# Two widths of matmul, and a planned order, changed in a two-layer mixer block on one core

## The chip, the core and the metric

The kernel runs on one core of one Trainium2 chip. A core has a matrix engine (PE, with its weight loads shown apart as PEld), a vector engine (DVE), a scalar engine (ACT), GpSimd (POOL) and a queue engine (SP) that issues the DMAs here. The metric is device time in microseconds, from the start to the end of one execution; lower is better.

## What is computed

Two layers of a mixer block on 512 latent tokens and 256 context tokens, 1024 wide. Each layer projects the modulated input into three branches (retention `r`, gated MLP `m`, differential attention `d`), gates each branch, projects each back to 1024 columns, merges them with sigmoid gates and applies an output projection:

```
h  = modulate(rms_norm(x), shift, scale)
z  = h @ w_in                       # keys, values, queries, gates, u, v, merge logits
o_ret  = from_heads(rms_norm(bidir_retention(rq, rk, rv)))  * silu(rg)
o_diff = from_heads(rms_norm(diff_attend(dq, dk, dv, lam))) * silu(dg)
o_mlp  = mu * spatial_mix(layer_norm(mv)) * silu(mg)
y   = sigmoid(l_r)*(o_ret @ w_bo[0]) + sigmoid(l_m)*(o_mlp @ w_bo[1]) + sigmoid(l_d)*(o_diff @ w_bo[2])
x   = x + gate * rms_norm(y @ w_out, g_post)
```

In layer 0 all 768 tokens go through everything. In layer 1 the context tokens only give keys and values, so most stages there have 512 tokens.

## The kernel before

Every projection is a product of two float32 numbers that are each kept as a high and a low part in a rounded 32-bit type (`HH` and `HL` for the input, a ring of two slots for weights). One product is therefore three matmuls per 128 rows of the contraction: high by high, high by low, low by high. All of them are recorded from line 314.

There are two kinds of projection. In `xs` tokens are the stationary side: one call makes 128 tokens by 256 output columns, with 24 matmuls of 256 columns. In `ws` weights are the stationary side: 128 output channels by a span of tokens. The gates (`dg`, `rg`), the merges (`dm`, `rm`, `mm`), and `mg` and `mu` of the gated MLP use `ws`. In layer 0 such a call is made for two spans, tokens 512 to 767 first (matmuls of 256 columns) and then tokens 0 to 511 (512 columns). A merge step has 36 matmuls for each span (24 for the logits, 12 for the branch), a gate step 24. `spans`, `cm_tiles`, `gate`, `merge` and `mlp` hold this.

The `v` projection of the gated MLP (`mv0`, `mv1`, columns 0 to 255 and 256 to 511) goes through `main_pairs`, first all token tiles with `mv0`, then all with `mv1`. The output projection (`out_phase`) takes four blocks of 256 columns, `wo0` to `wo3`, one after the other for each token tile.

Weights are loaded by `w_dma` into one of two raw buffers and divided by `w_split` into high and low part, in four pieces of 512 words: one ACT copy and one DVE subtraction each. `begin` splits a block and, ahead of time, the next one. Results lie in the eight PSUM banks of 512 words.

The attention and retention units (`d_unit`, tags `dat`; `r_state` and `r_attn`, tags `rst` and `rat`) are small matmuls with long chains on ACT and DVE between them. They are put in a list of side work and taken from it by `pop`, between the projections. One attention unit writes scores into the three banks `Sb`; DVE takes their maximum (`red`, line 370), ACT makes two exponentials from them, and only then may the next unit write its scores.

The order on each engine is not the order of the code. `Rec` records every operation with a cost; `schedule` plans time with these costs and with `LATENCY`, the time from an engine's end to another's start, and at each moment gives an engine the ready operation with the lowest place in the code (`prio`, which `bump` shifts). Engines then run strictly in that planned order.

Of the kernel before, what the change touches and what calls it, by code (L numbers as in the profile page):

```python
# [12 lines left out]
ALU = mybir.AluOpType  # L13
# [3 lines left out]
NT = NL + NCX  # L17
# [169 lines left out]
class Op:  # L187
# [4 lines left out]
LATENCY = {("PE", "ACT"): 200, ("PE", "DVE"): 200, ("PE", "SP"): 200, ("ACT", "PE"): 290, ("ACT", "DVE"): 100, ("ACT", "POOL"): 100,  # L192
           ("ACT", "SP"): 100, ("ACT", "ACT"): 100, ("DVE", "PE"): 290, ("DVE", "ACT"): 150, ("DVE", "POOL"): 170, ("DVE", "DVE"): 127,
           ("DVE", "SP"): 100, ("POOL", "PE"): 150, ("POOL", "ACT"): 65, ("POOL", "DVE"): 65, ("POOL", "POOL"): 102, ("POOL", "SP"): 100}
# [4 lines left out]
class Rec:  # L199
# [144 lines left out]
    def copy_v(self, out, in_):  # L344
        v = self.nc.vector
        c = self.n(in_) / (0.96 if self.ps(in_) or self.ps(out) else 1.92) + 160
        return self.add("DVE", lambda: v.tensor_copy(out, in_), [out], [in_], c)

    def tt(self, out, a, b, op):
        v = self.nc.vector  # L350
        return self.add("DVE", lambda: v.tensor_tensor(out, a, b, op=op), [out], [a, b], self.n(out) / 0.97 + 168)  # L351

    def ts(self, out, a, s1, s2=None, op0=ALU.mult, op1=None):
        v = self.nc.vector
        ins = [a] + [s for s in (s1, s2) if s is not None and not isinstance(s, float)]
        c = self.n(out) * (1.04 if self.ps(a) else 0.52) + 160 + 60 * (len(ins) - 1)
        if op1 is None:
            f = lambda: v.tensor_scalar(out, a, s1, None, op0=op0)  # L358
        else:
            f = lambda: v.tensor_scalar(out, a, s1, s2, op0=op0, op1=op1)  # L360
        return self.add("DVE", f, [out], ins, c)

    def stt(self, out, a, s, b, op0, op1):
        v = self.nc.vector
        ins = [a, b] + ([] if isinstance(s, float) else [s])
        return self.add("DVE", lambda: v.scalar_tensor_tensor(out, a, s, b, op0=op0, op1=op1), [out], ins, self.n(out) / 0.97 + 215)  # L366

# [12 lines left out]
    def bn_stats(self, out, in_):  # L380
        v = self.nc.vector
        return self.add("DVE", lambda: v.bn_stats(out, in_), [out], [in_], self.n(in_) / 0.96 + 155)

    def bn_aggr(self, out, in_):
        v = self.nc.vector
        return self.add("DVE", lambda: v.bn_aggr(out, in_), [out], [in_], 172)

    def ptt(self, out, a, b, op):
        g = self.nc.gpsimd
        n = self.n(out)  # L390
        c = 600 + 150 * n if op == ALU.pow else 2.4 * n + 250
        return self.add("POOL", lambda: g.tensor_tensor(out, a, b, op=op), [out], [a, b], c)  # L392
# [169 lines left out]
WBUMP = -20  # L562
H_LO = 6144
# [7 lines left out]
class Prog:  # L571
# [444 lines left out]
    def h_unit(self, k, ts_, v):  # L1016
# [408 lines left out]
    def cm_tiles(self, l, W, X, n0, ps):  # L1425

        if ps[1] is not None:
            self.ws(ps[1], X, slice(NL, NT), W, n0)
        self.ws(ps[0], X, slice(0, NL), W, n0)

    def spans(self, l):
        return ((0, 0, NL), (1, NL, NT)) if l == 0 else ((0, 0, NL),)
# [6 lines left out]
    def gate(self, l, c):  # L1439
# [5 lines left out]
        for i in range(2):  # L1445
            self.begin(l, f"{c}g{i}")
            W = self.W(l, f"{c}g{i}")
            for j in range(2):
                ch = 2 * i + j
                R.tag = f"L{l}.{c}g{ch}"  # L1450
                ps = [self.P(NL), self.P(NCX, align=256) if l == 0 else None]
                self.cm_tiles(l, W, (self.HH, self.HL), 128 * j, [p.ap if p else None for p in ps])
# [12 lines left out]
    def merge(self, l, c, extra=None):  # L1465
# [9 lines left out]
        for i in range(8):  # L1475
# [4 lines left out]
            ps = [self.P(NL), None, self.P(NL), None]  # L1480
            x = None
            if l == 0:
                x = self.P(2, NCX)
                ps[1], ps[3] = _View(x[:, 0]), _View(x[:, 1])
# [3 lines left out]
            for v, a, b in reversed(self.spans(l)):  # L1488
                R.tag = f"L{l}.{c}m{i}"
                self.ws(ps[v].ap, (self.HH, self.HL), slice(a, b), Wl, 0)  # L1490
                self.ws(ps[2 + v].ap, self.OT, slice(a, b), Wb, 0)
                R.tag += ".ev"
                R.act(sg[:, a:b], ps[v].ap, AF.Sigmoid)
                R.tt(dst[:, a:b], ps[2 + v].ap, sg[:, a:b], ALU.mult)
# [15 lines left out]
    def mlp(self, l):  # L1510
# [7 lines left out]
        vn = [F(512) for _ in range(nt)]  # L1518
        for i in range(2):
# [32 lines left out]
        for i in range(2):  # L1552
            self.begin(l, f"mu{i}")
            W = self.W(l, f"mu{i}")
            for j in range(2):
                g = 2 * i + j
                R.tag = f"L{l}.mu{g}"
                sp = [self.P(NL), self.P(NCX, align=256) if l == 0 else None]
                ps = [self.P(NL), self.P(NCX, align=256) if l == 0 else None]
                with R.pe():  # L1560
                    for t in range(nt):
                        o = sp[0][:, 128 * t:128 * t + 128] if t < 4 else sp[1][:, 128 * (t - 4):128 * (t - 4) + 128]
                        R.mm(o, vn[t][:, 128 * g:128 * g + 128], wst[:, g], True, True)
                self.cm_tiles(l, W, (self.HH, self.HL), 128 * j, [p.ap if p else None for p in ps])
# [58 lines left out]
    def out_phase(self, l):  # L1623
# [5 lines left out]
        for gi, g in enumerate(gs):  # L1629
# [7 lines left out]
            if gi == 0:  # L1637
                pss = [self.P(DM, hi=3072), self.P(DM, hi=3072)]
                for b in range(4):
# [17 lines left out]
            else:  # L1657
                for j, t in enumerate(g):
                    end = t == gs[-1][1]
                    if end and last:  # L1660

                        ps = self.P(3, 512)
                        pq = [ps[:, (0, 0, 1, 2)[b], 256 * (b == 1):256 * (b == 1) + 256] for b in range(4)]
                    else:
                        ps = self.P(DM, lo=1024 if end else 0, hi=3072)
                        pq = [ps[:, 256 * b:256 * b + 256] for b in range(4)]
                    for b in range(4):
                        R.tag = f"L{l}.out{t}"
                        self.xs(pq[b], (yh, yl), slice(128 * j, 128 * j + 128), wos[b])
# [4 lines left out]
                    if end and last:  # L1674
                        self.tile_last(l, t, ps, [(ps[:, 0], 0, 512), (pq[2], 512, 768), (pq[3], 768, 1024)])
# [189 lines left out]
```

## Time and profile before

| | us |
|---|---|
| median of 3 runs (1535.66 to 1537.17) | 1536.49 |
| the profiled execution, whole | 1536.63 |
| its span, first to last instruction | 1534.9 |
| PE busy | 1505.0 |
| DVE busy | 799.0 |
| ACT busy | 602.3 |

An engine's busy time is the union of its instructions' shown lengths. A matmul's shown length is longer than its share of the engine's time, since matmuls are pipelined: their starts lie closer together than their ends suggest. What a matmul costs is read from the distance of starts. The page's sections and the answers of the trace name groups by line, engine, operation and tile; `AR` holds high and low parts, `AF` plain float32, `PSM` the PSUM.

### The profile page before, as it was taken

What the parts mean: (1) busy time and instruction counts of PE and PEld (TensorE: products, weight loads), DVE (VectorE), ACT (ScalarE), POOL (GpSimd) and SP (SyncE); (2) the same over time, 40 slices, a digit from 0 to 9 for tenths busy, and PEclk for the clock granted to TensorE, in tenths of its full rate; (3) what the DMA queues carried; (4) which work ended last, traced back from release to release, by engine and by line L of the source; (5) the groups of instructions that cost most, each with busy time, mean ns of one, the idle gap of its engine ahead of it and who ended that gap; (6) DMA issues with size and microseconds to landing.
All of it is one profiled execution on the core that took longest, in us unless ns stands there. A gap on an engine that the chain in (4) does not pass through costs nothing.

```text
span 1534.9 us, 23633 instructions
## 1 busy us (share of the span) xinstructions
PE 1505.0 (98%) x9544; PEld 1350.8 (88%) x9544; DVE 799.0 (52%) x1551; ACT 602.3 (39%) x1298; POOL 168.9 (11%) x187
## 2 busy tenths in 40 slices
PE   7999999999999999999999999999999999999998
PEld 4799998989888888989889999989988888898888
DVE  4457635655333872235874654674656434344452
ACT  6735543573222222222223463464455333332341
POOL 1212201110000011001000131111110000201000
PEclk9999999999999999999999999999999999999999
DMA  9441312111231442122563223241211332321331
GB/s 364 144 138 56 86 40 76 50 52 63 75 116 54 165 138 83 56 74 88 187 201 124 97 101 121 86 117 49 83 42 56 103 117 83 118 98 65 119 124 69
DMA packets 37710, 156.32 MB, mean 102 GB/s; under 512 B 5345, under 2 KB 6497, under 8 KB 31201
## 3 DMA queue, kind: packets, MB, share of 16 engines
q1 hardware_dynamic: 37600, 154.81, 30.0%
q8 instruction: 75, 1.23, 0.3%
q14 instruction: 35, 0.28, 0.1%
HBM read 132.77 MB, written 4.19 MB: 89 GB/s over the span
## 4 chain that ended last, share of the span: by engine, by line
PE 94%; issue 1%; DVE 1%; ACT 1%; DMA 0%; POOL 0%; SPq 0%; DVEq 0%; POOLq 0%; ACTq 0%
PE PSM L314 91%; PE PSM L318 3%; ACT AF L339 1%; DMA AF<-AF 0%; POOL AF L392 0%; DVE AR L351 0%; SPq L401 0%; DVE AF L351 0%; DVE AF L366 0%; DVE AF L370 0%; ACT AR L339 0%; DVE AF L360 0%; DVE AF L378 0%; DVEq L1861 0%; POOLq L1861 0%
## 5 line engine op out<-in xcount | busy, mean ns | idle before, releaser
L314 PE MATMUL PSM<-AR 128*128 128x256 f32 (+1 forms) x8016 | 1361.8, 330 | 9.1 <-ACT AF L339 7.3
L314 PEld LDWEIGHTS PSM<-AR 128*128 128x128 f32 x8016 | 1186.5, 190 | 140.7 <-ACT AF L339 9.6
L339 ACT ACTIVATE AR<-AF 128x512 fp32r<-128x512 f32 (+4 forms) x489 | 285.2, 607 | 422.3 <-PE PSM L314 295.9
L351 DVE TENSOR_TENSOR AR<-AF,AR 128x512 fp32r<-128x512 f32 (+4 forms) x486 | 318.6, 673 | 252.6 <-ACT AR L339 205.2
L339 ACT ACTIVATE AF<-PSM 128x512 f32<-128x512 f32 (+4 forms) x385 | 170.5, 462 | 392.1 <-PE PSM L314 324.3
L392 POOL TENSOR_TENSOR AF<-AF 128x1 f32<-128x1 f32 (+5 forms) x180 | 168.2, 943 | 1360.9 <-DVE AF L360 588.5
L351 DVE TENSOR_TENSOR AF<-PSM,AF 128x512 f32<-128x512 f32 (+2 forms) x253 | 144.7, 581 | 236.6 <-PE PSM L314 111.8
L314 PE MATMUL PSM<-AF 128*128 128x128 f32 (+3 forms) x1104 | 143.9, 304 | 12.4 <-DMA AF<-wmodn 8.9
L314 PEld LDWEIGHTS PSM<-AF 128*128 128x128 f32 (+1 forms) x1104 | 127.2, 184 | 23.9 <-DVE AF L360 9.3
L339 ACT ACTIVATE AF<-PSM,AF 128x768 f32<-128x768 f32 (+2 forms) x144 | 91.9, 648 | 64.9 <-DVE AF L358 40.5
L374 DVE CUSTOM_DVE_ANT_0 AR<-AF 128x1024 fp32r<-128x1024 f32 x59 | 76.5, 1296 | 14.8 <-DMA AF<-wmod 8.8
L370 DVE TENSOR_REDUCE AF<-PSM 128x2 f32<-128x1536 f32 (+1 forms) x40 | 61.4, 1541 | 35.7 <-PE PSM L314 35.6
L360 DVE TENSOR_SCALAR AF<-AF 128x1 f32<-128x1 f32 (+3 forms) x188 | 42.5, 237 | 61.5 <-ACT AF L339 58.3
L318 PE MATMUL PSM<-AF 128*128 128x128 f32 x424 | 67.5, 277 | 2.1 <-DVE AF L366 1.2
L339 ACT ACTIVATE AF<-AF 128x256 f32<-128x256 f32 (+4 forms) x107 | 54.7, 558 | 20.4 <-POOL AF L392 10.3
L318 PEld LDWEIGHTS PSM<-AF 128*128 128x128 f32 x424 | 51.2, 142 | 13.1 <-ACT AF L339 3.2
L351 DVE TENSOR_TENSOR AF<-AF 128x512 f32<-128x512 f32 (+5 forms) x78 | 42.9, 555 | 13.2 <-PE PSM L318 5.0
L366 DVE SCALAR_TENSOR_TENSOR AF<-AF 128x768 f32<-128x768 f32 (+2 forms) x48 | 43.5, 913 | 3.6 <-POOL AF L392 2.7
L366 DVE SCALAR_TENSOR_TENSOR AF<-AF,PSM 128x128 f32<-128x128 f32 x64 | 19.8, 344 | 20.5 <-PE PSM L314 12.0
L358 DVE TENSOR_SCALAR AF<-AF 128x2 f32<-128x2 f32 (+4 forms) x98 | 20.4, 223 | 7.0 <-PE PSM L314 3.4
L360 DVE TENSOR_SCALAR AF<-PSM,AF 128x128 f32<-128x128 f32 x48 | 15.9, 404 | 12.0 <-PE PSM L318 11.9
L351 DVE TENSOR_TENSOR AR<-PSM,AR 64x256 fp32r<-64x256 f32 x24 | 10.1, 421 | 21.2 <-ACT AR L339 21.0
(20 smaller groups left out, 94.3 us busy)
## 6 DMA issues: line engine op xcount, KB each, us to landing
AF<-w SPq DMA_DIRECT2D x50, 1024.0 KB, 4.8
AF<-w SPq DMA_DIRECT2D x48, 768.0 KB, 4.2
AF<-wmod SPq DMA_DIRECT2D x32, 512.0 KB, 3.6
AF<-wmodn SPq DMA_DIRECT2D x16, 512.0 KB, 8.9
AF<-x SPq DMA_DIRECT2D x12, 512.0 KB, 4.2
AR<-AR SPq DMA_DIRECT2D x16, 384.0 KB, 4.6
AF<-AF SPq DMA_DIRECT2D x64, 64.0 KB, 2.3
AR<-AF SPq DMA_DIRECT2D x12, 256.0 KB, 2.3
```

Source lines behind the costliest of these rows:

```text
L314: self.add("PE", lambda: pe.matmul(out, lhsT, rhs, start=start, stop=stop), [out], [lhsT, rhs], c)
L318: self.add("PE", lambda: pe.transpose(out, in_, ident), [out], [in_, ident], 109.0)
L339: return self.add("ACT", lambda: e.activation(out, in_, func, **kw), outs, ins, c, tab)
L351: return self.add("DVE", lambda: v.tensor_tensor(out, a, b, op=op), [out], [a, b], self.n(out) / 0.97 + 168)
L358: f = lambda: v.tensor_scalar(out, a, s1, None, op0=op0)
L360: f = lambda: v.tensor_scalar(out, a, s1, s2, op0=op0, op1=op1)
L366: return self.add("DVE", lambda: v.scalar_tensor_tensor(out, a, s, b, op0=op0, op1=op1), [out], ins, self.n(out) / 0.97 + 215)
L370: return self.add("DVE", lambda: v.tensor_reduce(out, in_, axis=AX.X, op=op), [out], [in_], self.n(in_) / 0.96 + 155)
L374: return self.add("DVE", lambda: v.tensor_tensor_reduce(junk, a, b, 1.0, 0.0, ALU.mult, ALU.add, accum), [junk, accum], [a, b], self.n(a) ...
L392: return self.add("POOL", lambda: g.tensor_tensor(out, a, b, op=op), [out], [a, b], c)
```

## The change

Five things are changed.

1. In layer 0 the spans of `ws` are tokens 0 to 383 and 384 to 767, so that all its matmuls have 384 columns. Each span has a bank of its own (`banks`).
2. `v` projection: the first pair of token tiles is done as before, with `mv0` and then `mv1`; every further tile is done at once for both, with matmuls of 512 columns. Their moving side are two halves of 256 words from the two ring slots (`w_both`). `mv1` no longer splits the next block ahead, since that block's slot is still in use; the last tile is recorded in four groups of two rows of the contraction.
3. Output projection: blocks 0 and 1, and 2 and 3, are taken together in 512 columns in the same way, but for the first pair's blocks 0 and 1 and for the last tile's blocks 2 and 3.
4. The costs in `Rec` and the table `LATENCY` have new numbers: costs are smaller by 40 to 150 ns, the times from ACT or DVE to PE by 137 and 153 ns.
5. Side work is recorded with `ABUMP = -100`, which lets its operations go ahead of up to 100 others in the planner's choice.

```diff
-LATENCY = {("PE", "ACT"): 200, ("PE", "DVE"): 200, ("PE", "SP"): 200, ("ACT", "PE"): 290, ("ACT", "DVE"): 100, ("ACT", "POOL"): 100,
+LATENCY = {("PE", "ACT"): 200, ("PE", "DVE"): 200, ("PE", "SP"): 200, ("ACT", "PE"): 153, ("ACT", "DVE"): 133, ("ACT", "POOL"): 177,
...
-        c = self.n(in_) / 1.19 + (160 if self.ps(in_) else 195) + 198 * (accum is not None) + 60 * (len(ins) - 1)
+        c = self.n(in_) / 1.19 + (60 if self.ps(in_) else 95) + 150 * (accum is not None) + 88 * (len(ins) - 1)
...
+ABUMP = -100
...
-            self.w_split(i + 1)
+            if name != "mv1":
+                self.w_split(i + 1)
...
+        self.R.bump = ABUMP
         f()
+        self.R.bump = 0
...
+    def w_both(self, off, step):
+        a = self.AR[:, off:off + 2 * step].rearrange("p (a b) -> p a b", a=2)[:, :, 0:2048]
+        return a.rearrange("p a (k n) -> p k a n", k=KT)
...
+        for v, a, b in reversed(self.spans(l)):
+            self.ws(ps[v].ap, X, slice(a, b), W, n0)
+
+    def banks(self, l):
+        return [self.P(b - a, align=512) for v, a, b in self.spans(l)]
 
     def spans(self, l):
-        return ((0, 0, NL), (1, NL, NT)) if l == 0 else ((0, 0, NL),)
+        return ((0, 0, NT // 2), (1, NT // 2, NT)) if l == 0 else ((0, 0, NL),)
...
-            self.main_pairs(l, f"mv{i}", PAIRS if l == 0 else LATP, post)
+            self.main_pairs(l, f"mv{i}", prs[:1], post)
+        W = [self.w_both(RING[0] + 2048 * i, RING[1] - RING[0]) for i in range(2)]
+        for t in [t for pr in prs[1:] for t in pr]:
+            R.tag = f"L{l}.mv.{t}"
+            ps = self.P(2, 256)
+            for k in (0, 2, 4, 6) if t == prs[-1][1] else (None,):
+                self.xs(ps.ap, (self.HH, self.HL), slice(128 * t, 128 * t + 128), W, k if k is None else (k, k + 2))
+            R.copy_a(vn[t].ap, ps.ap.rearrange("p a b -> p (a b)"))
...
+                half = [[self.w_both(RING[0] + 2048 * x, RING[1] - RING[0]) for x in range(2)],
+                        [self.w_both(Z + 6144 * x, 2048) for x in range(2)]]
...
+                    if b == 2:
+                        continue
...
-                            self.xs(pss[j][:, 256 * b:256 * b + 256], (yh, yl), slice(128 * j, 128 * j + 128), wos[b], ks)
+                            o = pss[j][:, 512:1024].rearrange("p (a b) -> p a b", a=2) if b == 3 else pss[j][:, 256 * b:256 * b + 256]
+                            self.xs(o, (yh, yl), slice(128 * j, 128 * j + 128), half[1] if b == 3 else wos[b], ks)
```

What stands on PE at two places follows. In these rows `AR` matmuls belong to projections, or to the scores of an attention unit where they come as 2, 4 and 2; L318 are transposes, and `AF` matmuls of L314 products of the attention units or of retention.

PE in layer 0, late in the attention of head 3, before: the scores of one unit (the rows 512, 256, 256, 512), and from the eighth row on the scores of the next.

```order
L314 MATMUL PSM<-AR 128x512 x2
L314 MATMUL PSM<-AR 128x256 x2
L318 MATMUL PSM<-AF 128x128
L314 MATMUL PSM<-AF 128x128 x2
L314 MATMUL PSM<-AR 128x256 x2
L314 MATMUL PSM<-AR 128x512 x2
L318 MATMUL PSM<-AF 128x128 x8
L314 MATMUL PSM<-AR 128x512 x2
L314 MATMUL PSM<-AR 128x256 x2
```

The same two units of the same head on PE in the changed kernel:

```order
L314 MATMUL PSM<-AR 128x512 x2
L314 MATMUL PSM<-AR 128x256 x4
L314 MATMUL PSM<-AR 128x512 x2
L314 MATMUL PSM<-AR 128x256 x24
L318 MATMUL PSM<-AF 128x128
L314 MATMUL PSM<-AF 128x128 x6
L314 MATMUL PSM<-AR 128x256 x24
L318 MATMUL PSM<-AF 128x128 x7
L314 MATMUL PSM<-AR 128x512 x2
L314 MATMUL PSM<-AR 128x256 x4
L314 MATMUL PSM<-AR 128x512 x2
```

Between the two units' scores stood eight transposes; now there stand two projections of 24 matmuls, eight transposes and six products.

PE at the end of layer 0 before: the last merge step (36 and 36), the output projection, and in between the transposes (eight for a token tile) that bring a finished tile into the next layer.

```order
L314 MATMUL PSM<-AR 128x256 x36
L314 MATMUL PSM<-AR 128x512 x36
L314 MATMUL PSM<-AR 128x256 x264
L318 MATMUL PSM<-AF 128x128 x8
L314 MATMUL PSM<-AR 128x256 x24
L318 MATMUL PSM<-AF 128x128 x4
L314 MATMUL PSM<-AR 128x256 x24
L318 MATMUL PSM<-AF 128x128 x4
L314 MATMUL PSM<-AR 128x256 x72
L318 MATMUL PSM<-AF 128x128 x8
```

The same place in the changed kernel:

```order
L314 MATMUL PSM<-AR 128x384 x132
L314 MATMUL PSM<-AR 128x256 x96
L314 MATMUL PSM<-AR 128x512 x72
L318 MATMUL PSM<-AF 128x128 x8
L314 MATMUL PSM<-AR 128x512 x24
L318 MATMUL PSM<-AF 128x128 x8
L314 MATMUL PSM<-AR 128x512 x48
L318 MATMUL PSM<-AF 128x128 x8
```

The merge runs in one width, and the output projection in 512 columns after its first 96 matmuls.

## Rows read from the trace of the kernel before

**Rows 1.** The page: busy time and share by engine; granted clock, 40 slices.

```profile
PE 1505.0 (98%) x9544; PEld 1350.8 (88%) x9544; DVE 799.0 (52%) x1551; ACT 602.3 (39%) x1298; POOL 168.9 (11%) x187
...
PEclk9999999999999999999999999999999999999999
```

**Rows 2.** Groups by form on PE, whole span: busy us, mean ns; idle.

```profile
L314 PE MATMUL PSM<-AR 128*128 128x512 f32 x3344 | 799.3, 393 | 3.6 <-ACT AF L339 3.6
L314 PE MATMUL PSM<-AR 128*128 128x256 f32 x4672 | 590.3, 284 | 5.5 <-ACT AF L339 3.7 <-DVE AF L351 1.6
```

**Rows 3.** The same view of 618 to 646 us, and of 1205 to 1250.

```profile
L314 PE MATMUL PSM<-AR 128*128 128x256 f32 x236 | 28.5, 283 | 0.0
...
L314 PE MATMUL PSM<-AR 128*128 128x512 f32 x200 | 45.5, 389 | 0.0
```

**Rows 4.** The same view, at 522.59 (256 after 512) and 526.90 (512 after 256).

```profile
L314 PE MATMUL PSM<-AR 128*128 128x256 f32 x1 | 0.3, 278 | 0.0
...
L314 PE MATMUL PSM<-AR 128*128 128x512 f32 x1 | 0.4, 396 | 0.0
```

**Rows 5.** Timeline of PE, first stage (two halves of 256): start us, us.

```profile
42.65 1.64 PE L314 MATMUL PSM<-AR 128*128 128x512 f32 x6
...
44.48 2.32 PE L314 MATMUL PSM<-AR 128*128 128x512 f32 x9
```

**Rows 6.** Waits of PE, 60 to 1200 us: us in total, times, longest.

```profile
PE PSM L314 <- ACT AF L339: 9.1, 8, 2.5
PE PSM L314 <- DVE AF L351: 1.6, 1, 1.6
PE PSM L318 <- DVE AF L366: 1.2, 3, 0.5
PE PSM L318 <- ACT AF L339: 0.5, 1, 0.5
```

**Rows 7.** Timeline at 308 us, attention of layer 0, head 3; idle in brackets.

```profile
308.30 1.04 PE L318 MATMUL PSM<-AF 128*128 128x128 f32 x8
308.50 1.76 DVE L370 TENSOR_REDUCE AF<-PSM 128x2 f32<-128x1536 f32 x1 [1.52 <-PE PSM L314]
...
310.79 0.91 ACT L339 ACTIVATE AF<-PSM,AF 128x768 f32<-128x768 f32 x1
...
311.85 0.97 PE L314 MATMUL PSM<-AR 128*128 128x512 f32 x4 [2.51 <-ACT AF L339]
```

**Rows 8.** Timeline of PE, attention of layer 1, head 3.

```profile
1139.48 1.39 PE L314 MATMUL PSM<-AR 128*128 128x512 f32 x4 [1.12 <-ACT AF L339]
...
1143.77 1.60 PE L314 MATMUL PSM<-AF 128*128 128x128 f32 x12 [0.90 <-ACT AF L339]
...
1147.34 1.13 PE L318 MATMUL PSM<-AF 128*128 128x128 f32 x7 [0.37 <-DVE AF L366]
```

**Rows 9.** Timeline of PE, attention of layer 1, head 1.

```profile
1030.62 0.97 PE L314 MATMUL PSM<-AR 128*128 128x256 f32 x4 [1.08 <-ACT AF L339]
...
1033.95 1.60 PE L314 MATMUL PSM<-AF 128*128 128x128 f32 x12 [0.90 <-ACT AF L339]
```

**Rows 10.** Timeline of ACT, end of layer 0: finishing tile 4, and weight pieces.

```profile
844.91 1.02 ACT L339 ACTIVATE AF<-PSM 128x1024 f32<-128x1024 f32 x1 [11.61 <-PE PSM L314]
...
848.80 1.02 ACT L339 ACTIVATE AR<-AF 128x256 fp32r<-128x256 f32 x3
...
850.77 1.63 ACT L339 ACTIVATE AR<-AF 128x256 fp32r<-128x256 f32 x5
...
853.39 2.10 ACT L339 ACTIVATE AF<-AF 128x1024 f32<-128x1024 f32 x2 [0.99 <-POOL AF L392]
```

**Rows 11.** The page: two costliest groups of weight splitting; DMA of weight blocks.

```profile
L339 ACT ACTIVATE AR<-AF 128x512 fp32r<-128x512 f32 (+4 forms) x489 | 285.2, 607 | 422.3 <-PE PSM L314 295.9
L351 DVE TENSOR_TENSOR AR<-AF,AR 128x512 fp32r<-128x512 f32 (+4 forms) x486 | 318.6, 673 | 252.6 <-ACT AR L339 205.2
...
AF<-w SPq DMA_DIRECT2D x50, 1024.0 KB, 4.8
```

More of the change, by code (lines that the diff above doesn't have):

```diff
@@ L188 @@
     pass
-LATENCY = {("PE", "ACT"): 200, ("PE", "DVE"): 200, ("PE", "SP"): 200, ("ACT", "PE"): 290, ("ACT", "DVE"): 100, ("ACT", "POOL"): 100,
-           ("ACT", "SP"): 100, ("ACT", "ACT"): 100, ("DVE", "PE"): 290, ("DVE", "ACT"): 150, ("DVE", "POOL"): 170, ("DVE", "DVE"): 127,
-           ("DVE", "SP"): 100, ("POOL", "PE"): 150, ("POOL", "ACT"): 65, ("POOL", "DVE"): 65, ("POOL", "POOL"): 102, ("POOL", "SP"): 100}
+LATENCY = {("PE", "ACT"): 200, ("PE", "DVE"): 200, ("PE", "SP"): 200, ("ACT", "PE"): 153, ("ACT", "DVE"): 133, ("ACT", "POOL"): 177,
+           ("ACT", "SP"): 135, ("ACT", "ACT"): 135, ("DVE", "PE"): 137, ("DVE", "ACT"): 119, ("DVE", "POOL"): 163, ("DVE", "DVE"): 117,
+           ("DVE", "SP"): 117, ("POOL", "PE"): 93, ("POOL", "ACT"): 73, ("POOL", "DVE"): 73, ("POOL", "POOL"): 102, ("POOL", "SP"): 100}
 WINDOW = 3413.3
@@ L345, in copy_v @@
         v = self.nc.vector
-        c = self.n(in_) / (0.96 if self.ps(in_) or self.ps(out) else 1.92) + 160
+        c = self.n(in_) / (0.96 if self.ps(in_) or self.ps(out) else 1.92) + 76
         return self.add("DVE", lambda: v.tensor_copy(out, in_), [out], [in_], c)
@@ L350, in tt @@
         v = self.nc.vector
-        return self.add("DVE", lambda: v.tensor_tensor(out, a, b, op=op), [out], [a, b], self.n(out) / 0.97 + 168)
+        return self.add("DVE", lambda: v.tensor_tensor(out, a, b, op=op), [out], [a, b], self.n(out) / 0.97 + 84)
     def ts(self, out, a, s1, s2=None, op0=ALU.mult, op1=None):
@@ L355, in ts @@
         ins = [a] + [s for s in (s1, s2) if s is not None and not isinstance(s, float)]
-        c = self.n(out) * (1.04 if self.ps(a) else 0.52) + 160 + 60 * (len(ins) - 1)
+        c = self.n(out) * (1.04 if self.ps(a) else 0.52) + 76 + 60 * (len(ins) - 1)
         if op1 is None:
@@ L390, in ptt @@
         n = self.n(out)
-        c = 600 + 150 * n if op == ALU.pow else 2.4 * n + 250
+        c = 560 + 150 * n if op == ALU.pow else 2.4 * n + 210
         return self.add("POOL", lambda: g.tensor_tensor(out, a, b, op=op), [out], [a, b], c)
@@ L1450, in gate @@
                 R.tag = f"L{l}.{c}g{ch}"
-                ps = [self.P(NL), self.P(NCX, align=256) if l == 0 else None]
-                self.cm_tiles(l, W, (self.HH, self.HL), 128 * j, [p.ap if p else None for p in ps])
+                ps = self.banks(l)
+                self.cm_tiles(l, W, (self.HH, self.HL), 128 * j, ps)
                 sg = F(n)
@@ L1479, in merge @@
             Wb = self.W(l, f"{c}m{i}", 128, 1024, 4)
[L1480 to L1484, printed above, removed]
+            ps, pb = self.banks(l), self.banks(l)
             sg = F(n)
@@ L1490, in merge @@
                 self.ws(ps[v].ap, (self.HH, self.HL), slice(a, b), Wl, 0)
-                self.ws(ps[2 + v].ap, self.OT, slice(a, b), Wb, 0)
+                self.ws(pb[v].ap, self.OT, slice(a, b), Wb, 0)
                 R.tag += ".ev"
                 R.act(sg[:, a:b], ps[v].ap, AF.Sigmoid)
-                R.tt(dst[:, a:b], ps[2 + v].ap, sg[:, a:b], ALU.mult)
+                R.tt(dst[:, a:b], pb[v].ap, sg[:, a:b], ALU.mult)
                 if last:
@@ L1501, in merge @@
             sg.free()
-            for p in (ps[0], ps[2], x):
-                if p is not None:
-                    p.free()
+            for p in (*ps, *pb):
+                p.free()
             if extra:
@@ L1518, in mlp @@
         vn = [F(512) for _ in range(nt)]
+        prs = PAIRS if l == 0 else LATP
         for i in range(2):
@@ L1522, in post @@
                     R.copy_a(vn[t][:, 256 * i:256 * i + 256], ps[:, j])
-            self.main_pairs(l, f"mv{i}", PAIRS if l == 0 else LATP, post)
+            self.main_pairs(l, f"mv{i}", prs[:1], post)
[6 more added lines that the diff above has]
+            R.copy_a(vn[t].ap, ps.ap.rearrange("p a b -> p (a b)"))
+            ps.free()
+            self.step()
         R.tag = f"L{l}.ln"
@@ L1540, in mlp @@
                 R.tag = f"L{l}.mg{2 * i + j}"
-                ps = [self.P(NL), self.P(NCX, align=256) if l == 0 else None]
-                self.cm_tiles(l, W, (self.HH, self.HL), 128 * j, [p.ap if p else None for p in ps])
+                ps = self.banks(l)
+                self.cm_tiles(l, W, (self.HH, self.HL), 128 * j, ps)
                 s = F(n)
@@ L1557, in mlp @@
                 R.tag = f"L{l}.mu{g}"
-                sp = [self.P(NL), self.P(NCX, align=256) if l == 0 else None]
-                ps = [self.P(NL), self.P(NCX, align=256) if l == 0 else None]
+                sp, ps = self.banks(l), self.banks(l)
                 with R.pe():
                     for t in range(nt):
-                        o = sp[0][:, 128 * t:128 * t + 128] if t < 4 else sp[1][:, 128 * (t - 4):128 * (t - 4) + 128]
+                        v, a, b = self.spans(l)[t // 3 if l == 0 else 0]
+                        o = sp[v][:, 128 * t - a:128 * t - a + 128]
                         R.mm(o, vn[t][:, 128 * g:128 * g + 128], wst[:, g], True, True)
-                self.cm_tiles(l, W, (self.HH, self.HL), 128 * j, [p.ap if p else None for p in ps])
+                self.cm_tiles(l, W, (self.HH, self.HL), 128 * j, ps)
                 f = F(n)
@@ L1662, in out_phase @@
                         ps = self.P(3, 512)
-                        pq = [ps[:, (0, 0, 1, 2)[b], 256 * (b == 1):256 * (b == 1) + 256] for b in range(4)]
+                        po = [(ps[:, 0].rearrange("p (a b) -> p a b", a=2), half[0]), (ps[:, 1, 0:256], wos[2]), (ps[:, 2, 0:256], wos[3])]
                     else:
                         ps = self.P(DM, lo=1024 if end else 0, hi=3072)
-                        pq = [ps[:, 256 * b:256 * b + 256] for b in range(4)]
-                    for b in range(4):
+                        po = [(ps[:, 512 * b:512 * b + 512].rearrange("p (a b) -> p a b", a=2), half[b]) for b in range(2)]
+                    for b, (o, w) in enumerate(po):
                         R.tag = f"L{l}.out{t}"
-                        self.xs(pq[b], (yh, yl), slice(128 * j, 128 * j + 128), wos[b])
+                        self.xs(o, (yh, yl), slice(128 * j, 128 * j + 128), w)
                         if end and not last and b == 0:
```

17 lines of the change are left out of this document (7 added, 10 removed).

## The prediction

> **What bounds the kernel now.** I read the page first. PE is busy for 1505.0 of 1534.9 us, no other engine for more than about half, and the granted clock is full in all 40 slices, that is 2.4 GHz [rows 1]. So time can only go where PE spends it: in the number and width of its matmuls, or in the gaps between them. Two forms make up nearly all of it, 4672 matmuls of 256 columns and 3344 of 512 [rows 2]. Their lengths overlap, so the cost is the distance of starts: in a stretch of one form, busy time less one length, over the count less one. That is (28.5 - 0.283)/235 = 120.0 ns for 256 columns and (45.5 - 0.389)/199 = 226.7 ns for 512 [rows 3]. The two forms come to 560.6 + 758.1 = 1319 us. One column costs less in a wide matmul: 0.443 ns against 0.469.
>
> The gaps are few. Between 60 and 1200 us PE is seen waiting 13 times, 12.4 us in all [rows 6]. A gap only shows once it outlasts the overlap of two bars, 283 - 120 = 163 ns, so 13 x 0.163 = 2.1 us are hidden and the waits are worth about 14.5 us. All of the large ones lie in the two attention stretches. Outside them nothing waits, so other engines' work in merges and gates is hidden.
>
> **The change part by part.** The sum is made against the profiled execution, 1536.6 us, which is 0.1 us from the median of the runs.
>
> *256 to 512 columns.* `v` projection: 96 matmuls fewer in layer 0 (four tiles), 48 in layer 1 (two tiles). Output projection: 48 + 192 in layer 0 (first pair, four tiles), 48 + 48 + 24 in layer 1 (first pair, a tile, half of the last). Together 504 fewer. Each replaces 2 x 120.0 by 226.7, if two halves of 256 words stream like one piece of 512. The first stage has such matmuls already: three more of them take 2.32 - 1.64 = 0.68 us, 227 ns each [rows 5]. The gain is 504 x 13.3 ns = **6.7 us**. The rows are rounded to 10 ns, 3 ns over three matmuls, which gives 5 to 8.4 us.
>
> *512 and 256 to 384 columns.* 24 merge steps of 36, eight gate steps of 24, eight steps each of 24 in `mg` and `mu` (four and four channels): 864 + 192 + 192 = 1248 pairs. A pair costs 226.7 + 120.0 = 346.7 ns now. No row has a matmul of 384, so its cost lies between the neighbours, 120.0 and 226.7, which would be a gain or a loss of up to 1248 x 106.7 = 133 us. The straight line between the two points gives 173.3 and no gain; 512's price per column gives 170.0 and a gain of 6.7 ns a pair. I take 170.0, for this reason. A matmul of 256 in a row of its like is shown with 283 ns, the first one behind a matmul of 512 with 278 [rows 3, 4]. The first 512 behind 256s is shown with 396, one in a row of 512s with 389. So something that a predecessor of 226.7 covers and one of 120.0 doesn't (the weight load, which goes beside it) adds 5 to 7 ns. Without it 256 columns would cost about 113, which is 512's price per column. A 384 has a predecessor of 170, well over 120, and should be free of it. Gain: 1248 x 6.7 ns = **8.3 us**, with 0 as the near bound.
>
> On the length of a bar the Trainium skill says (Perfetto Trace Analysis, the section on the Tensor Engine under "Per-instruction lifecycle") that a matmul's start is the start of its operand fetch and its end an estimate. By that the 5 to 7 ns are partly a model; no sum changes, but the straight line keeps a fair chance.
>
> *The waits.* The largest is of this kind: the next attention unit's scores need DVE's maximum (1.76 us) and ACT's exponential (0.91) of the last, 3.4 us from 308.5 to 311.85, while only eight transposes (1.04) stand between: 2.51 us idle [rows 7]. In the new order there stand 48 matmuls of 256 (5.8 us), eight transposes (0.9) and six products (1.3): 8.0 us for the same 3.4. The next place is head 3 of layer 1, 1.12 + 0.90 + 0.37 [rows 8]; the new order puts 48 matmuls of a projection between those scores. Head 1 of layer 1, 1.08 + 0.90 [rows 9], gets 24 matmuls of 512, 5.4 us. These six waits, 6.9 us and 1.0 hidden, should go: 7.9 us. Of the other seven (6.6 us) I take half, 3.3, since the planner's numbers now fit the trace better: five copies of 256 on ACT take 1.63 us, three 1.02, so one 305 ns [rows 10], where the old cost is 410 and the new 310. Gain **11.2 us**, at most 14.5. Against it stand new waits: attention is denser now and has less slack from step to step. Nothing shows them; I take **1 us**, and the far end is that all the waits only move.
>
> *Steps with little cover, costed at nothing.*
> - `mg0` can only be split once the last `v` tile has left its slot. That tile's four groups free it quarter by quarter, every 6 x 0.227 = 1.4 us; the last quarter needs a copy and a subtraction, at most 0.61 + 0.67 = 1.3 us [rows 11], while 18 matmuls of `mg0` (3.1 us) can run without it. If layer norm holds ACT or DVE up, up to four pieces are late, 4 x 0.61 + 0.67 = 3.1 us in each layer.
> - `mv1` is first used 48 matmuls (5.8 us) after its slot comes free, 144 (17.3 us) before. Its split takes 3.1 us.
> - `wo3` is wanted behind two column blocks (11.5 us) instead of three (17.3). Its DMA can be issued once `wo1` has left the raw buffer, lands after 4.8 us and is split in 3.1 [rows 11]: 7.9 us behind the split of `wo1`, which itself ends 1 to 3 us into the phase. The margin is 0.6 to 2.6 us, SP has nothing else queued there, and a miss costs about 1 us in each layer.
> - Finishing tile 4 takes 9.5 us from its last matmul to its normalized copy, 844.91 to 854.44 [rows 10]. Before, 96 matmuls of 256 hid it (11.5 us), now 48 of 512 (10.9).
> - In layer 0 the `d` gate has only two banks, since the attention buffers hold six. One span now takes one and the other span the other, 4.1 us each, and emptying a bank needs one ACT and one DVE operation, at most 1.3 us by rows 11.
>
> *Sum.* 1536.6 - 6.7 - 8.3 - 11.2 + 1.0 = **1511.4 us**. The start (DMAs, the first stage) and the last tile's chain are as before.
>
> **The rivals.**
> - *A matmul has a fixed price beside its columns* (the straight line): 13.3 ns each, whatever its width. For it: two points fit it exactly. Against it: rows 4. Then 384 gains nothing: **1519.7 us**.
>  The Trainium skill has a rule of this form (TensorE: Matmul & The Clock Gate, section "Back-to-back issue gap"): columns over 2.4 plus 2.5 ns. By it 256 and 512 would take 109.2 and 215.8 ns, the 384s would gain nothing and the 512s 504 x 2.5 ns = 1.3 us. The trace disagrees on the constant, 120.0 and 226.7, and the measurement decides; on the form it can't tell.
> - *The waits only move.* The new plan sets attention steps closer together, and each can wait a little for ACT or DVE. For it: all 13 waits lie in chains of this kind. Against it: 4.6 us of slack at the largest place. **1521.6 us**; with the straight line as well, **1529.9**.
> - *Slower: a matmul of 384 occupies PE longer than its columns say*, at worst like one of 512. The price is 1248 x 2 x the excess. The other terms bring 16.9 us, so from 180 ns a matmul on (170.0 forecast) the kernel is slower, and at 226.7 it takes **1653 us**. For it: no row excludes it. Against it: two widths that are both about proportional.
> - That the change doesn't do what it says is out: the built order has 2496 matmuls of 384, 2600 of 512 and 2416 of 256, 504 fewer than before.
>
> **How the numbers follow.** Forecast 0.62, fixed price 0.20, moved waits 0.10, both 0.04, slower 0.04. The low end takes all 14.5 us of waits and no new one, 8.4 for the 512s and about 1 us of gaps too short to be seen: 1504. The high end is moved waits with `mg0` or `wo3` late by 2 to 3 us: 1524. Outside are "both", "slower" and parts of the rest, under 0.2. A measurement can tell 0.2%, 3.1 us, from no change. Faster by more than that are all cases but the slower one and, where new waits add to "both", 0.03 of that: faster 0.93, same 0.03, slower 0.04.
>
> **What would show it.** In a merge of layer 0 the distance of starts for 384 columns: 170 (forecast), 173 (fixed price), over 180 (slower). A merge step of 72 should take 12.24 us instead of 12.48. In the `v` stage 226 to 229 ns for 512. In the attention stretches the list of waits should hold 2 to 5 us instead of 12.4, with nothing near 2.5; a sum near 12 means moved waits. PE idle just ahead of the first `mg0` or of the first 512s of the output projection would show the thin covers. A wrong 384 price is the one thing that could turn the sign.

## The result, and the profile after

The changed kernel takes 1518.38 us (median of 4 runs, 1517.28 to 1519.65), the kernel before beside it 1536.83: a ratio of 0.988, 95% interval 0.9863 to 0.9897. That is 18.4 us faster. The forecast was 1511.4 us, and the rival with a fixed price per matmul 1519.7. The profiled execution took 1517.34 us with a span of 1515.5, against 1536.63 and 1534.9.

The page of the changed kernel, busy time of PE and granted clock, answers to [rows 1]:

```profile
PE 1493.6 (99%) x9040; PEld 1372.6 (91%) x9040; DVE 797.2 (53%) x1551; ACT 600.3 (40%) x1292; POOL 170.4 (11%) x187
...
PEclk9999999999999999999999999999999999999999
```

504 matmuls are gone, and PE is still what bounds the kernel, at full clock. The forms on PE over the whole span (busy us, mean ns of one, idle before) answer to [rows 2]:

```profile
L314 PE MATMUL PSM<-AR 128*128 128x512 f32 x2600 | 624.2, 394 | 0.7 <-DVE AF L351 0.7
L314 PE MATMUL PSM<-AR 128*128 128x384 f32 x2496 | 437.8, 335 | 0.0
L314 PE MATMUL PSM<-AR 128*128 128x256 f32 x2416 | 310.7, 284 | 0.0
```

The same view of a stretch of merges in layer 0 (520 to 600 us), and of the `v` stage (612 to 640 us):

```profile
L314 PE MATMUL PSM<-AR 128*128 128x384 f32 x464 | 80.6, 334 | 0.0
...
L314 PE MATMUL PSM<-AR 128*128 128x512 f32 x89 | 20.4, 389 | 0.0
```

Read as in the prediction, a matmul of 384 columns costs (80.6 - 0.334)/463 = **173.4 ns**, and one of 512 from two halves (20.4 - 0.389)/88 = 227.4 ns. The first is the number of the straight line, the second is as forecast.

Last, the waits of PE from 60 to 1200 us (us in total, times, longest), which answer to [rows 6]:

```profile
PE PSM L318 <- ACT AF L339: 2.2, 4, 1.0
PE PSM L314 <- DVE AF L351: 0.7, 1, 0.7
```

12.4 us in 13 waits have become 2.9 us in five. So the time came from fewer matmuls and from vanished waits. The new width gave nothing.

### The profile page after: what moved, and what is told of

It is laid out like the page before. It is cut to its first block, busy times and chain, and to the rows that moved or that the text cites. A ratio compares the mean times of both kernels' runs of the same rounds, so it can differ in the third digit from the quotient of the medians.

```text
span 1515.5 us, 22649 instructions
## 1 busy us (share of the span) xinstructions
PE 1493.6 (99%) x9040; PEld 1372.6 (91%) x9040; DVE 797.2 (53%) x1551; ACT 600.3 (40%) x1292; POOL 170.4 (11%) x187
## 4 chain that ended last, share of the span: by engine, by line
PE 94%; DVE 2%; issue 1%; DMA 1%; POOL 1%; ACT 0%; SPq 0%; DVEq 0%; POOLq 0%; ACTq 0%
PE PSM L314 91%; PE PSM L318 3%; POOL AF L392 1%; DVE AR L351 0%; ACT AF L339 0%; DVE AF L351 0%; DMA AF<-AF 0%; SPq L401 0%; DMA AF<-w 0%; DVE AF L360 0%; DVE AF L370 0%; DVE AF L366 0%; ACT AR L339 0%; DVEq L1885 0%; POOLq L1885 0%
## 5 line engine op out<-in xcount | busy, mean ns | idle before, releaser
L314 PE MATMUL PSM<-AR 128*128 128x384 f32 (+2 forms) x7512 | 1354.5, 339 | 0.7 <-DVE AF L351 0.7
L314 PEld LDWEIGHTS PSM<-AR 128*128 128x128 f32 x7512 | 1208.5, 189 | 100.9 <-issue 1.2
L351 DVE TENSOR_TENSOR AR<-AF,AR 128x512 fp32r<-128x512 f32 (+3 forms) x486 | 316.5, 668 | 231.1 <-ACT AR L339 193.3
L392 POOL TENSOR_TENSOR AF<-AF 128x128 f32<-128x128 f32 (+5 forms) x180 | 169.7, 951 | 1340.0 <-DVE AF L351 533.0
L339 ACT ACTIVATE AF<-PSM 128x256 f32<-128x256 f32 (+5 forms) x379 | 169.9, 467 | 356.4 <-PE PSM L314 321.3
L351 DVE TENSOR_TENSOR AF<-PSM,AF 128x512 f32<-128x512 f32 (+3 forms) x253 | 144.8, 581 | 256.2 <-PE PSM L314 160.4
L314 PE MATMUL PSM<-AF 128*128 128x128 f32 (+3 forms) x1104 | 142.0, 300 | 11.8 <-DMA AF<-wmodn 9.6
L314 PEld LDWEIGHTS PSM<-AF 128*128 128x128 f32 (+1 forms) x1104 | 127.0, 184 | 21.3 <-DVE AF L360 9.4
L318 PE MATMUL PSM<-AF 128*128 128x128 f32 x424 | 67.7, 277 | 3.2 <-ACT AF L339 3.2
L318 PEld LDWEIGHTS PSM<-AF 128*128 128x128 f32 x424 | 51.1, 141 | 14.2 <-ACT AF L339 6.4
L382 DVE BATCH_NORM_STATS2 AF<-AF 128x6 f32<-128x512 f32 x10 | 6.7, 691 | 37.6 <-ACT AF L339 37.5
L366 DVE SCALAR_TENSOR_TENSOR AF<-AF,PSM 128x128 f32<-128x128 f32 x64 | 19.9, 344 | 12.4 <-PE PSM L314 6.1
```

The source lines that it names most:

```text
L314: self.add("PE", lambda: pe.matmul(out, lhsT, rhs, start=start, stop=stop), [out], [lhsT, rhs], c)
L318: self.add("PE", lambda: pe.transpose(out, in_, ident), [out], [in_, ident], 109.0)
```

## The experiments

Ratios are against the kernel before, run beside each; its median was 1536.8 us each time.

### The spans of layer 0 back to 512 and 256 columns

```diff
-        return ((0, 0, NT // 2), (1, NT // 2, NT)) if l == 0 else ((0, 0, NL),)
+        return ((0, 0, NL), (1, NL, NT)) if l == 0 else ((0, 0, NL),)
...
-                        v, a, b = self.spans(l)[t // 3 if l == 0 else 0]
+                        v, a, b = self.spans(l)[t // 4]
```

> The changed kernel with the spans of layer 0 put back to 512 and 256 columns; all else as in the changed kernel. Forecast's theory (384 columns at 170.0 ns): the 1248 pairs cost 346.7 instead of 340.0 ns again, so 8.3 us slower than the changed kernel, 1526.7 us. Rival (fixed price per matmul, 384 at 173.3 ns): no difference, 1518.4 us, within 1.5 us.

Measured: 1519.86 us, ratio 0.9883 (0.987 to 0.9897), the changed kernel's own ratio to 0.0003. The 8.3 us of the forecast's price do not show. By medians it is 1.5 us slower, and the two intervals lie on each other. 384 columns for 512 and 256 are worth nothing that can be measured here.

### The widths alone, with the old plan

```diff
-LATENCY = {("PE", "ACT"): 200, ("PE", "DVE"): 200, ("PE", "SP"): 200, ("ACT", "PE"): 153, ...
+LATENCY = {("PE", "ACT"): 200, ("PE", "DVE"): 200, ("PE", "SP"): 200, ("ACT", "PE"): 290, ...
...
-ABUMP = -100
+ABUMP = 0
```

The costs in `Rec` are the old ones too.

> The changed kernel with the planner's old costs and latencies and without the shift of side work: the new widths alone. Fixed price per matmul: only the 504 matmuls saved, 6.7 us, so 1530 us, and waits of the matrix engine between 60 and 1200 us stay near 12 us. Forecast's price of 384: 15 us, 1521.6. If the waits go with the new widths themselves and not with the plan: 1518 to 1520 us with waits near 3 us.

Measured: 1529.04 us, ratio 0.9947 (0.9934 to 0.9959), 7.7 us faster than before. The list of waits from 60 to 1200 us is line by line that of [rows 6]: 9.1, 1.6, 1.2 and 0.5 us, in the same numbers of times. So the widths take away no wait at all, and their 7.7 us (6.3 to 10.1 by the interval) are the 504 saved matmuls, put at 6.7.

### The order alone, with the old widths

The kernel before with the new `LATENCY`, the new costs and `ABUMP = -100`.

> The kernel before with the planner's new costs and latencies and the shift of side work by 100, all widths as before: the order alone. If the waits go because of the new plan: 11 to 13 us off, 1524 to 1526 us, and the waits of the matrix engine between 60 and 1200 us sum to 2 to 4 us. Rival (the waits go only together with the new widths): under 3 us off, 1534 us or more, and waits of 9 us or more.

Measured: 1524.84 us, ratio 0.992 (0.9907 to 0.9934), 11.9 us faster than before. The waits of PE from 60 to 1200 us:

```profile
PE PSM L318 <- ACT AF L339: 1.2, 3, 0.5
PE PSM L314 <- DVE AF L351: 0.6, 1, 0.6
```

1.8 us in four waits, for 12.4 in 13. With the 0.163 us that each wait hides, that is 10.6 + 9 x 0.163 = 12.1 us, and 11.9 were measured. The two parts of the change add up: 7.7 + 11.9 = 19.6 us, against 18.4 for both.

### The new costs without the shift, and the shift without the costs

The first is the kernel before with the new `LATENCY` and costs. The second is the kernel before with this alone:

```diff
+ABUMP = -100
...
+        self.R.bump = ABUMP
         f()
+        self.R.bump = 0
```

> The kernel before with the planner's new costs and latencies, without the shift of side work. Theory A (new costs that fit the chip take the waits away): 8 us or more of the 11.9 us of the order alone, so 1525 to 1529 us, waits of the matrix engine between 60 and 1200 us under 5 us. Theory B (the shift of side work does it): under 3 us off, 1534 us or more, waits of 10 us or more.

> The kernel before with side work shifted ahead by 100, without the new costs. Theory A (the new costs do it): under 3 us off, 1534 us or more, waits of 10 us or more between 60 and 1200 us. Theory B (the shift does it): 1525 to 1529 us, waits under 5 us.

Measured: the costs alone 1529.39 us, ratio 0.9952 (0.994 to 0.9965), 7.4 us faster. The shift alone 1539.45 us, ratio 1.0019 (1.0011 to 1.0028), slower. The waits of PE from 60 to 1200 us, costs alone:

```profile
PE PSM L318 <- ACT AF L339: 2.4, 3, 1.4
PE PSM L314 <- ACT AF L339: 0.9, 1, 0.9
PE PSM L314 <- DVE AF L351: 0.6, 1, 0.6
PE PSM L318 <- DVE AF L366: 0.6, 2, 0.4
```

And the shift alone:

```profile
PE PSM L314 <- ACT AF L339: 9.2, 7, 2.6
PE PSM L314 <- DVE AF L351: 2.8, 2, 1.6
PE PSM L318 <- ACT AF L339: 0.9, 1, 0.9
PE PSM L318 <- DVE AF L366: 0.2, 1, 0.2
```

4.5 us against 13.1. The costs alone fall just short of what theory A asked (8 us, 1529 us at most). A plan with the old costs has the wait of 2.51 us at head 3 [rows 7] with the shift too (2.6 here). With the new costs, a smaller step (11.9 - 7.4 = 4.5 us) comes from the shift, which is worth nothing by itself. A likely reason, not tested further, is that being allowed ahead only helps where the planner knows the time at which that pays.

The shift alone lost time in one more way. Stretches of a microsecond in layer 1, head 3 (length, busy time and instructions of PE, PEld, DVE, ACT and POOL, then the granted clock as a share of full speed, and DMA):

```profile
1140.00:1141.00 1.00, 0.37 (x4) 0.13 (x2) 0.00 (x0) 0.70 (x1) 0.00 (x0) 1.00 0.00 0
1141.00:1142.00 1.00, 0.65 (x3) 0.66 (x4) 0.53 (x3) 0.46 (x3) 0.00 (x0) 0.83 0.00 0
1142.00:1143.00 1.00, 0.79 (x3) 0.07 (x2) 1.00 (x2) 0.00 (x0) 0.00 (x0) 0.50 0.00 0
```

The granted clock falls from 2.4 to 1.2 GHz after two waits of PE, 1.74 us before 1139.29 and 0.97 before 1141.35, and is full again from 1149. Twelve products at that clock, on the timeline of PE:

```profile
1145.42 2.93 PE L314 MATMUL PSM<-AF 128*128 128x128 f32 x12 [0.90 <-ACT AF L339]
```

The same twelve took 1.60 us before [rows 8]. Of this kernel's 11 executions the one with a mean granted clock of 0.999 took 1537.34 us, and the ten with 0.995 to 0.997 took 1538.70 to 1540.72. By that one execution the shift alone would be about even at the full clock, against 1536.84 before.

### The old times between engines under the new costs

The changed kernel with the old `LATENCY`; costs and shift stay new.

> The changed kernel with the old table of times between engines, and all else, the new costs of single operations and the shift of side work, as in the changed kernel. Theory A (the shorter costs of operations took the waits away): 1518 to 1520 us, waits of the matrix engine between 60 and 1200 us under 4 us. Theory B (the shorter times from the scalar and vector engines to the matrix engine did it): 5 us or more come back, 1523 us or more, waits of 6 us or more.

Measured: 1523.88 us, ratio 0.9921 (0.9904 to 0.9937), 5.5 us slower than the changed kernel. The waits of PE from 60 to 1200 us:

```profile
PE PSM L318 <- ACT AF L339: 4.2, 4, 2.1
PE PSM L318 <- DVE AF L366: 1.0, 3, 0.4
PE PSM L314 <- ACT AF L339: 0.9, 1, 0.9
PE PSM L314 <- DVE AF L351: 0.5, 1, 0.5
```

6.6 us in nine waits. That is theory B's 5 us and waits above 6. But theory A isn't wrong altogether: with the old times between engines, the new costs and the shift, about half of the 12.4 us is still gone. So the new costs of operations and the shift are not enough for the whole gain. What the new times between engines would bring with the old costs was not run.

### Matmuls by width, alone

Rows of 64 matmuls, one width on each line of the code, all in the high parts' type, for instance:

```python
for i in range(N):
    pe.matmul(PSM[:, 1536:1920], W[i % 8], X[:, 0:384], start=i == 0, stop=i == N - 1)
```

> All of the model's computation is left out; rows of 64 matmuls each in one width stand one after the other, to read the distance of starts by width. Fixed price per matmul, (columns + 32) over 2.4 GHz: 512 at 226.7 ns, 448 at 200.0, 384 at 173.3, 320 at 146.7, 256 at 120.0, and 512 and 256 taken by turns 346.7 a pair. Forecast's theory (the price is a weight load that a long predecessor covers): 448 at 198.3, 384 at 170.0, 320 at 141.7, 256 at 120.0. With weights of 64 or 32 columns: if the constant is the matmul's own, 512 stays at 226.7; if it is the weight load's, 220 and 216.7. For 192 and 128 columns: 93.3 and 66.7 by the fixed price, or a floor of about 110 to 120 ns if a weight load can't go faster.

The timeline of PE (start us, us; 128*64 and 128*32 are weights of 64 and 32 columns):

```profile
21.58 14.67 PE L1852 MATMUL PSM<-AR 128*128 128x512 f32 x64
36.09 13.13 PE L1854 MATMUL PSM<-AR 128*128 128x448 f32 x64
49.06 11.28 PE L1856 MATMUL PSM<-AR 128*128 128x384 f32 x64
60.18 9.54 PE L1858 MATMUL PSM<-AR 128*128 128x320 f32 x64
69.56 7.84 PE L1860 MATMUL PSM<-AR 128*128 128x256 f32 x64
77.23 7.29 PE L1862 MATMUL PSM<-AR 128*128 128x192 f32 x64
84.36 7.28 PE L1864 MATMUL PSM<-AR 128*128 128x128 f32 x64
91.48 14.90 PE L1866 MATMUL PSM<-AR 128*64 128x512 f32 x64
106.22 15.00 PE L1868 MATMUL PSM<-AR 128*32 128x512 f32 x64
...
135.57 11.47 PE L1874 MATMUL PSM<-AR 128*128 128x512 f32 x64
146.88 14.68 PE L1876 MATMUL PSM<-AR 128*128 128x512 f32 x64
```

From one line's start to the next, over 64: 226.7 ns for 512 columns, 202.7 for 448, 173.8 for 384, 146.6 for 320, 119.8 for 256. Four of the five lie on columns plus 32 over 2.4 GHz within 0.5 ns; 448 is 2.7 above it. 192 and 128 columns both cost 111 ns, a floor. With weights of 64 columns 512 rises to 230.3, where one theory expected 226.7 and the other 220.

L1874 takes 512 and 256 columns by turns; its row names only the first form. Its 32 pairs cost (146.88 - 135.57)/32 = 353.4 ns each, where both theories expected 346.7. So a matmul of 512 ahead of one of 256 doesn't make the pair cheaper, and changing width at every matmul costs 6.7 ns a pair that neither theory has. The projections of the kernel before change width only between blocks of 24 or 36, so this weighs little there.

The Trainium skill says (TensorE: Matmul & The Clock Gate, the section "Step-by-step: what each phase is for") that the next weights load while the current matmul runs. For 512 columns these rows agree: lighter weights save nothing. For 256 the next kernel doesn't quite: with half the weight columns 6 ns of 120 go.

### The weights of a matmul of 384

The same kind of kernel, with weights of 128, 96, 64 and 32 columns.

> All of the model's computation is left out; rows of 64 matmuls each, in 256, 320, 384, 448 and 512 columns with weights of 128, 96, 64 or 32 columns, and three rows with the same weights every time. Theory A (a part of the price is the weight load, also at 384): 256 falls from 120.0 to 113.3 ns with weights of 64 columns, and 384 falls from 173.3 to about 170, which is 512's price per column. Theory B (the price of 384 is its own): 384 stays at 173.3 ns with weights of 96, 64 and 32 columns. With the same weights every time both expect no change, since each matmul still has its load.

Its timeline of PE:

```profile
43.08 11.25 PE L1856 MATMUL PSM<-AR 128*64 128x384 f32 x64
54.17 11.25 PE L1858 MATMUL PSM<-AR 128*32 128x384 f32 x64
65.27 7.83 PE L1860 MATMUL PSM<-AR 128*128 128x256 f32 x64
...
80.36 7.42 PE L1864 MATMUL PSM<-AR 128*64 128x256 f32 x64
87.61 9.54 PE L1866 MATMUL PSM<-AR 128*64 128x320 f32 x64
```

384 columns cost 11.09/64 = 173.3 ns with weights of 64 columns and 173.4 with 32, about the same as with 128 (173.8); with 96 they cost 174.8, 1.5 more than theory B's 173.3. 256 columns fall from 119.7 to 113.3 with 64. In the rows with the same weights every time nothing changes, as both theories expected: 119.7 for 256 columns, 173.4 for 384, 227.3 for 512. Theory B holds for 384 in that lighter weights take nothing off its price. And the constant is not the same thing at every width. Narrower weights also write fewer rows of the PSUM, so that the 6.4 ns at 256 columns belong to the load alone is likely and not shown.

### One group for the last tile of the `v` projection

```diff
-            for k in (0, 2, 4, 6) if t == prs[-1][1] else (None,):
+            for k in (None,):
```

> The changed kernel with the last tile of the v projection in one group instead of four in both layers, so that its weight slots come free at its end and not quarter by quarter. Forecast's step on thin cover: the first piece of the next block needs a copy and a subtraction, 0.61 + 0.67 us and the way to them, so the matrix engine waits some 1.5 us ahead of mg0 in each layer: 3 us slower than the changed kernel, 1521.5 us. Rival (the order is planned around it, or the slot comes free early anyway): no wait there, 1518.4 us.

Measured: 1521.04 us, ratio 0.9898 (0.9884 to 0.9911), 2.7 us slower than the changed kernel. The timeline of ACT and of PE at the end of the stage in layer 0 (in brackets the idle time before, and what ended it):

```profile
643.72 0.60 ACT L339 ACTIVATE AF<-PSM 128x512 f32<-128x512 f32 x1 [4.84 <-PE PSM L314]
644.22 4.27 ACT L339 ACTIVATE AR<-AF 128x512 fp32r<-128x512 f32 x8
644.89 0.62 PE L314 MATMUL PSM<-AR 128*128 128x384 f32 x2 [1.20 <-ACT AR L339]
```

All pieces of `mg0` (`AR<-AF`) stand behind the copy of the last tile, and PE waits 1.20 us for the first of them. In layer 1 the same edit costs no wait, and ACT shows why:

```profile
1350.25 0.63 ACT L339 ACTIVATE AR<-AF 128x512 fp32r<-128x512 f32 x1 [0.81 <-PE PSM L314]
1351.62 0.63 ACT L339 ACTIVATE AR<-AF 128x512 fp32r<-128x512 f32 x1 [0.74 <-PE PSM L314]
1352.92 0.63 ACT L339 ACTIVATE AR<-AF 128x512 fp32r<-128x512 f32 x1 [0.67 <-PE PSM L314]
1354.28 0.60 ACT L339 ACTIVATE AF<-PSM 128x512 f32<-128x512 f32 x1 [0.73 <-PE PSM L314]
```

Three pieces stand ahead of that copy, and each starts some 1.35 us after the one before, which is six matmuls of 512. They are released inside the one group. So a group doesn't hold a slot back on the chip here. It only moves the planned place of the pieces in ACT's queue, and where a copy that waits for the tile's end is ahead of them, they wait with it. The trace accounts for 1.4 us of waits (1.20 and one of 0.18) and some 0.3 hidden; the rest of the 2.7 is not found, and is about the scatter of the runs. That the time came so near the 3 us expected is therefore partly chance: one of the two waits expected is there, not both.

### Two blocks more in 512 columns, and finishing work ahead

```diff
+        W = [self.w_both(RING[0] + 2048 * i, RING[1] - RING[0]) for i in range(2)]
+        for t in range(4):
...
+            ps = self.P(2, 256, hi=1024)
...
+        R.bump = FBUMP
         R.act(u.ap, ps.ap, AF.Square, accum=s[:, 0:1])
         self.rstd(s[:, 1:2], s[:, 0:1], 1.0 / DM, EPS)
```

> The changed kernel, with two additions. In layer 1 dv0 and rkv0 are taken together in 512 columns as mv0 and mv1 are, four tiles, 96 matmuls fewer: by the fixed price 13.3 ns each, 1.3 us. And the operations that finish a token tile go ahead of up to 100 others in the planner's choice, so that the small operation ahead of the wait of 0.96 us at 852 us is not queued behind eight scalings: 0.96 + 0.16 us if that wait goes. Together 2.4 us faster than the changed kernel, 1516.0 us. Rival (new waits in the start of layer 1, where one span of two halves holds back the next block's split): 1518 us or more, with waits seen after the 512s there.

Measured: 1515.72 us, ratio 0.9867 (0.9852 to 0.9883), 2.7 us faster than the changed kernel by medians, where 2.4 were expected; the two intervals overlap. Its waits from 60 to 1200 us are 1.9 us. In the changed kernel, PE waited ahead of the transposes of tile 5 (timeline of DVE, POOL, ACT and PE):

```profile
845.62 2.64 DVE L360 TENSOR_SCALAR AF<-PSM,AF 128x128 f32<-128x128 f32 x8 [0.34 <-PE PSM L318]
...
848.18 0.14 DVE L360 TENSOR_SCALAR AF<-AF 128x1 f32<-128x1 f32 x1
...
848.40 2.80 POOL L392 TENSOR_TENSOR AF<-AF 128x1 f32<-128x1 f32 x1 [6.58 <-DVE AF L360]
851.24 1.15 ACT L339 ACTIVATE AF<-AF 128x1024 f32<-128x1024 f32 x1 [1.88 <-POOL AF L392]
...
852.44 1.09 PE L318 MATMUL PSM<-AF 128*128 128x128 f32 x8 [0.96 <-ACT AF L339]
```

With the finishing work ahead:

```profile
845.37 1.05 DVE L360 TENSOR_SCALAR AF<-PSM,AF 128x128 f32<-128x128 f32 x3 [0.34 <-PE PSM L318]
...
846.33 0.14 DVE L360 TENSOR_SCALAR AF<-AF 128x1 f32<-128x1 f32 x1
...
846.55 0.55 POOL L392 TENSOR_TENSOR AF<-AF 128x1 f32<-128x1 f32 x1 [4.99 <-DVE AF L360]
847.14 1.15 ACT L339 ACTIVATE AF<-AF 128x1024 f32<-128x1024 f32 x1 [1.60 <-POOL AF L392]
...
851.06 1.03 PE L318 MATMUL PSM<-AF 128*128 128x128 f32 x8
```

The operation of 0.14 us stood behind eight scalings of tile 4, 2.56 us after the first of them. Now it stands behind three, 0.96 us after. POOL's power that follows is shown with 2.80 us in the one and 0.55 in the other; its spans are rough, and what made it long was not tried. Counted from the first scaling, the copy on ACT that the transposes need begins 3.9 us sooner (5.62 against 1.77), 1.6 of it by the place on DVE and 2.25 by POOL's shorter time, and PE no longer waits. By these prices 1.1 us of the gain is this wait with what it hides, and 96 x 13.3 ns = 1.3 us the saved matmuls; the two were not run apart. By its median this kernel beats both others.

## Why the prediction was right, and where it was not

The measured 1518.4 us lies within the range given, 1504 to 1524, and 7.0 us above the forecast. Nearly all of that is one term, the 8.3 us of the 384s, less 1.0 us that the 512s and 0.6 us that the waits brought beyond their forecast.

*256 to 512 columns*: 6.7 us forecast, 7.7 measured by the widths alone, whose merges also run at 173.4 ns and gain nothing. The reason holds: 227.4 ns in the `v` stage, as in [rows 5].

*512 and 256 to 384*: 8.3 us forecast, nothing found. This is the step that failed: "A 384 has a predecessor of 170, well over 120, and should be free of it." The reading behind it was half right. The few ns that [rows 4] show at 256 columns fit the weight load, since 256 columns cost 113.3 ns with half the weight columns. That a long predecessor covers them is not borne out: 512 and 256 by turns cost 353.4 ns a pair. And the two known widths can't tell whether 384 lies on 512's price per column or on the line between them, and 384 has its 173 to 175 ns with any weights. Two points fit a line exactly whatever lies between them; more than bounds the rows did not give. The rival took the line as it stood and came out at 1519.7, 1.3 us from the result. Why 384 costs 3.3 ns more than 512's price per column, and 448 2.7 more than the line, stays open.

*The waits*: 11.2 us gained and 1 lost, 10.2 net. The trace gives 12.4 - 2.9 = 9.5 us shown and 8 x 0.163 = 1.3 hidden, 10.8 net, and the order alone 11.9. All six named waits of [rows 7 to 9] are gone; in layer 1's attention none is left. The net came out well because two misses offset each other. By place and operation none of the 13 waits is left, 14.5 us instead of 11.2, and the five waits now seen stand elsewhere. That the new numbers of the planner do it is shown: costs alone 7.4 us, the shift alone nothing. That they do it because they fit the trace better, the reason given, rests on few figures: the 305 ns of a copy, and a hand-over in [rows 7], where ACT's exponential ends at 311.70 and the scores start at most 0.15 us later (290 ns in the old table, 153 in the new). What the forecast did not say is that the shift needs the costs. The rival in which the waits only move is out.

*New waits*: 1 us forecast, and 2.9 us in five places found, 3.7 with what they hide. Four stand in layer 0 between 98 and 269 us (0.67, 0.48, 0.58 and 0.20 us); the largest, 0.96 us, is at the transposes of tile 5. That place had been looked at one tile too early: tile 4 was costed as thin cover [rows 10] and made it. Tile 5's chain, queued behind tile 4's scalings on DVE and then shown with 2.80 us on POOL, did not.

*The other thin covers*: `mg0`, `mv1`, `wo3` and the `d` gate cost nothing, as put down. PE runs through the end of the `v` stage and through the output projection without a wait except tile 5's. For `mg0` the cover was the right one but its mechanism was not: not the freeing of the slot by groups, but the place of its pieces in ACT's queue.

*The sum*: with the fixed price and the other terms as forecast, 1519.7; with the terms as the runs had them, 1536.8 - 7.7 - 10.8 = 1518.3, and 1518.4 was measured. That they meet to 0.1 us is chance, since the runs alone spread over 2.4 us.

## What to carry to other kernels

A price between two known widths isn't known from them; where a change hangs on a new width, measure that width alone first, or take the line and give the better price as the hope. In a kernel that one engine bounds at 98%, two things paid: fewer matmuls for the same columns, and new costs in the planner, nearer to the trace where that was looked at, which with the shift took away most of the waiting. A priority has to be judged together with the planner's costs: the same shift of side work gave 4.5 us with the new costs and lost 2.6 with the old ones.

## What was not expected of the hardware

- The constant beside a matmul's columns is not one thing at every width: with weights of 64 columns for 128, 256 columns get cheaper (119.7 to 113.3 ns), 384 stays (173.3), and 512 gets dearer (226.7 to 230.3). The Trainium skill (TensorE: Matmul & The Clock Gate, section "Back-to-back issue gap") gives one constant of 2.5 ns for the isolated gap of a matmul; here, in rows of matmuls, it is 13.3 ns at 256, 320, 384 and 512 columns.
- Below 256 columns the price stops falling: 111 ns for 192 and for 128.
- Two widths by turns cost more than the two in rows of their like: 353.4 ns for a pair of 512 and 256 columns, against 346.5.
- With the shift alone, the granted clock fell to half after two waits of 1.74 and 0.97 us with little work between them. In the kernel before, a single wait of 2.51 us at head 3 of layer 0 left it at 2.4 GHz, and so did 1.12 and 0.90 us with more work between them in layer 1 [rows 7, 8]. The executions in which the mean clock shows it took 1.4 to 3.4 us more than the one in which it doesn't.
